# A hybrid decoder layer: the first two weight tiles as one item, loads in a fixed order, joined final sums, and a longer distance from transposes to products

## The chip, the core and the metric

The kernel runs on one core of a Trainium2 chip. The metric is the device time of one execution in microseconds (us). A difference of about 0.2% can be told from no change.

The core's engines are TensorE (PE in the profile, its weight loads PEld), VectorE (DVE), ScalarE (ACT), GpSimd (POOL) and SyncE (SP). Each works through its own queue in order. Transfers are issued on a queue of SP, ACT or POOL and carried out by 16 DMA engines.

## The reference, cut to what matters

One layer (DEPTH = 1) on a residual stream x of 512 tokens by 1024 features, all in float32:

```
proj   = x @ w_in                       # q, k, v of three mixers, and three gate vectors
o_da   = differential attention         # 4 heads, two softmax maps each, RMSNorm per head
o_sb   = stick-breaking attention       # 8 heads, cumulative sums of log sigmoid(-z)
o_dl   = dilated window attention       # 3 groups x 4 heads, joined by their denominators
merged = sum_i sigmoid(gate_i) * (o_i @ w_branch_i)
x1     = LayerNorm(alpha * x + merged @ w_out)
hid    = square(relu(x1 @ w_up))        # 4096 wide
out    = LayerNorm(alpha * x1 + hid @ w_down + sigmoid(x1 @ w_ple_gate) * (p @ w_ple))
```

## The kernel before, in words

**Precision.** Each float32 operand of a large product is split in a rounded high part (h) and the rest (lo). A product is three matmuls: h by h, h by lo, lo by h. The high part is a copy on ScalarE (line 209 for weights), the rest a subtraction on VectorE (line 210). `split_psum`, `evac_stacked` and `evac_twice` (lines 100 to 133) do the same for results in PSUM; line 108 is their subtraction.

**Items.** The program is a list of items. An item has weight chunks, a function that issues its matmuls (`mm`) and one that evacuates the result (`ev`). The main loop (lines 1166 to 1201) issues, for item n: the evacuation of item n-1, some splits, a step of the attention heads, the matmuls of item n with another step in the middle, more splits. Matmul results take turns in two PSUM banks (`mm_bank`); heads, transposes and kept sums use six others (`at_bank`).

A `t_item` (line 243) makes 128 columns of the projection transposed: 24 matmuls of 512 columns. A group of four `v_items` makes values, token tile by token tile, 24 matmuls each, from four chunks. The order is that of `main_order`: two tiles sb_q 0 and sb_k 0, two tiles sb_q 1 and sb_k 1, the values sb_v, then the rest; three gate tiles of column group j are placed two groups ahead of the branch items that use them.

**Weights.** `load` and `fill` (lines 146 to 183) put 512 KB loads on SP's queue into a ring of four raw buffers. `issue_split` splits a chunk into one of seven pairs of buffers (`RING`). `pump(limit, most)` issues up to `most` splits, as far as the count of freed chunks allows. A chunk counts as freed by the item that is its last reader. x is loaded as eight pieces of 256 KB. The first tile's weights come as pieces of 128 KB and 384 KB between them, the second tile's as one chunk behind them.

**Heads.** Heads are generators; each `yield` ends a step, and the main loop calls `step()` twice for most items. So the yields set how many matmuls of items stand between a head's parts. `sb_head` (line 858) does logits (138, 139), ScalarE and VectorE passes (881 to 888), sums by triangular and all-ones matrices (895, 898) and the products with v (917, 919). `da_block` (line 935) does the logits, softmax passes, three yields, transposes (963) and their copy, one yield, the products with v (976); after a head's last block follow the norm, transposes (994) and a split. Before the third item of the first branch group all heads that are left are run to their end without items between (line 1170).

**The end.** The up projection feeds seven blocks of a seven-product scheme (`down`, lines 614 to 656; products 1, 6 and 7 stay in PSUM over all blocks, 2, 3, 4 and 5 are added on VectorE by line 638). The last eighth is done plainly (`plain`, lines 658 to 681): for each of four token tiles and two halves of columns 12 matmuls and an addition (674). After a tile's second half comes its layer norm: `layer_norm_act` (line 420) for tiles 0 to 2, with two sums (425) and two squares (429) on ScalarE, and `layer_norm` (405) for tile 3, with bn_stats on VectorE. Halves are stored on the ACT and SP queues (677).

**Start.** 14 matmuls on zeros (line 734) run first. Constants are made on POOL and cast on VectorE (741 to 758); seven small loads stand on POOL's queue (763, 820 to 838).

Of the kernel before, what the change touches and what calls it, by code (L numbers as in the profile page):

```python
# [17 lines left out]
P = 128  # L18
# [37 lines left out]
def trunk(tc, a, out):  # L56
    nc = tc.nc
    es = ExitStack()
    with es:
# [82 lines left out]
        RING, RAW, NSUM = 7, 4, 3  # L142
        loads, sums, chunks, placed = [], [], [], []
# [24 lines left out]
        def fill():  # L168
            while st["dma"] < len(loads):
                s = loads[st["dma"]]  # L170
                if not s["own"]:
                    if len(placed) >= RAW and placed[-RAW]["uses"]:
                        break
                    placed.append(s)
                if s["own"]:
                    s["raw"] = slot("rawx")
                else:
                    r = ring.tile([P, 1024], F32, name=nm("raw"), tag="raw", bufs=RAW)
                    s["raw"] = r[:, :s["w"]]
                nc.sync.dma_start(s["raw"], s["src"])  # L180
                st["dma"] += 1
                add()
            add()
# [12 lines left out]

        def issue_split():
            c = chunks[st["split"]]
# [8 lines left out]
            for h, lo, a0, a1 in parts:  # L207
                raw = c["from"]["raw"][:, a0:a1]
                nc.scalar.copy(h, raw)  # L209
                nc.vector.tensor_sub(lo, raw, h.bitcast(F32))  # L210
# [32 lines left out]
        def t_item(nt, name, j):  # L243
            w = a["wt"][nt]
            if nt == 0:
                x_chunk(0)
                c0 = chunk(w[:, 0:2, :].rearrange("p k m -> p (k m)"), 256)
                x_chunk(1)
                c1 = chunk(w[:, 2:8, :].rearrange("p k m -> p (k m)"), 768)
                for i in range(2, 8):  # L250
                    x_chunk(i)
                cs = [c0, c1]
            else:
                cs = [chunk(w.rearrange("p k m -> p (k m)"), 1024)]

            def mm(ps):
                for k in range(8):
                    c = cs[0] if nt or k < 2 else cs[1]
                    s = slice(k * P, k * P + P) if nt or k < 2 else slice(k * P - 256, k * P - 128)
# [3 lines left out]

            def ev(ps):
# [21 lines left out]
            item(cs, mm, ev)  # L286
# [33 lines left out]
        nt = nv = 0  # L320
        order = main_order()
        for kind, name, j in order:
# [24 lines left out]
        def branch_items(j):  # L347
            c1 = chunk(a["wb1"][j].rearrange("p k m -> p (k m)"), 1024)
            c2 = chunk(a["wb2"][j].rearrange("p k m -> p (k m)"), 512)
            for n, i in enumerate((1, 2, 0)):  # L350
                def mm(ps, i=i):
# [23 lines left out]
        first_branch = [None]  # L375
        LEAD = 2
# [6 lines left out]
        for j in range(8):  # L383
            branch_items(j)
            if j + LEAD < 8:
                for i in range(3):
                    t_item(nt, "gate", 8 * i + j + LEAD)
                    nt += 1
# [31 lines left out]
        def layer_norm_act(ts, g, b, fin):  # L420

            sm, sq = small("lsm", 2), small("lsq", 2)
            junk = slot("junk")
            for h in range(2):
                nc.scalar.activation(junk, ts[h], AF.Copy, accum_out=sm[:, h:h + 1])
# [129 lines left out]
        def mlp_items():  # L555
# [102 lines left out]
            def plain(cs):  # L658

                for tt in range(4):  # L660
                    for half in range(2):
                        def mm(ps, tt=tt, half=half):
                            q = slice(tt * P, tt * P + P)
                            for i in range(4):
                                h, lo = left[4 * nb + i]
                                c = cs[i % 2, half]
                                s = slice((i // 2) * 512, (i // 2) * 512 + 512)
                                nc.tensor.matmul(ps, h[:, q], c["h"][:, s], start=i == 0, stop=False)
                                nc.tensor.matmul(ps, h[:, q], c["l"][:, s], start=False, stop=False)
                                nc.tensor.matmul(ps, lo[:, q], c["h"][:, s], start=False, stop=i == 3)  # L670

                        def ev(ps, tt=tt, half=half):
                            t = acc[tt, half]
                            nc.vector.tensor_add(t, t, ps)
                            if half:
# [3 lines left out]
                                norm = layer_norm if tt == 3 else layer_norm_act  # L679
                                norm([acc[tt, 0], acc[tt, 1]], "ln2_g", "ln2_b", fin)  # L680
                        item(list(cs.values()) if (tt, half) == (3, 1) else [], mm, ev, need=list(cs.values()))
# [3 lines left out]
            for b in range(nb):  # L685
# [17 lines left out]
                down(b, 3, 0, c3)  # L703
                down(b, 1, 1, c1, [c1, cu])
                down(b, 6, 0, c6)
                down(b, 3, 1, c3, [c3])
# [3 lines left out]
                down(b, 2, 0, c2)  # L710
                down(b, 6, 1, c6, [c6, cu])
                down(b, 2, 1, c2, [c2])
# [3 lines left out]
                down(b, 4, 0, c4)  # L716
                down(b, 7, 0, c7)
                down(b, 7, 1, c7, [c7])
                down(b, 4, 1, c4, [c4])
            wd = a["wd"][nb]  # L720
            plain({(i // 2, i % 2): chunk(wd[i].rearrange("p k n -> p (k n)"), 1024) for i in range(4)})
# [11 lines left out]
        for i in range(14):  # L733
            nc.tensor.matmul(warm, zero[:, 0:P], zero, start=i == 0, stop=i == 13, skip_group_check=True)
        pump(8, 10)
# [5 lines left out]
        nc.vector.tensor_copy(identb, ident)  # L741
# [5 lines left out]
        nc.vector.tensor_copy(ones_r, ones_f)  # L747
# [4 lines left out]
        nc.vector.tensor_copy(tri_r, tri_f)  # L752
# [5 lines left out]
        nc.vector.tensor_copy(mask_b, mask_f)  # L758
# [4 lines left out]
        nc.gpsimd.dma_start(rel[0:32, :], a["rel"])  # L763
# [54 lines left out]
        lamt = slot("lamt")[:, :256].rearrange("p (a b) -> p a b", a=4)  # L818
        src = a["da_lambda"]
        nc.gpsimd.dma_start(lamt, bass.AP(tensor=src.tensor, offset=src.offset, ap=[[0, P], [64, 4], [1, 64]]))  # L820
        lp = one.tile([P, 2], F32, name="lp")
        for i in range(2):
            nc.vector.scalar_tensor_tensor(lamt[:, 2 * i, :], lamt[:, 2 * i, :], 1.0, lamt[:, 2 * i + 1, :],
                                           op0=OP.mult, op1=OP.mult, accum_out=lp[:, i:i + 1])
        nc.scalar.activation(lp, lp, AF.Exp)
        nc.vector.tensor_sub(lam, lp[:, 0:1], lp[:, 1:2])
        nc.vector.tensor_scalar(lam, lam, LAM_INIT, -1.0, op0=OP.add, op1=OP.mult)
        gcol = one.tile([P, 1], F32, name="gcol")
        nc.gpsimd.dma_start(gcol, a["da_norm"])
        nc.vector.tensor_scalar(gcol, gcol, 1.0 - LAM_INIT, None, op0=OP.mult)  # L830
        fold = one.tile([P, P], F32, name="fold")
        foldT = one.tile([P, P], F32, name="foldT")
        nc.gpsimd.dma_start(fold, a["perm"][:, 0:P])
        nc.gpsimd.dma_start(foldT, a["perm"][:, P:2 * P])
        exf = one.tile([P, 8], F32, name="exf")
        nc.gpsimd.dma_start(exf, a["exf"][:, 0:8])
        pick = one.tile([P, 64], F32, name="pick")
        nc.gpsimd.dma_start(pick, a["exf"][:, 8:72])
# [19 lines left out]
        def sb_head(hd):  # L858
# [18 lines left out]
            for bi in (2, 1, 0):  # L877
# [5 lines left out]
                nc.scalar.activation(e, e, AF.Ln, bias=1.0)  # L883
# [4 lines left out]
                nc.vector.tensor_sub(lo, e, h.bitcast(F32))  # L888
# [32 lines left out]
            if 4 + pr not in oT:  # L921
# [4 lines left out]
            if side:  # L926
# [8 lines left out]
        def da_block(hd, qb):  # L935
# [31 lines left out]
            while ("da_v", 0, qb) not in V:  # L967
                yield
            if hd not in da_po:
# [196 lines left out]
        for n, it in enumerate(items):  # L1166
# [3 lines left out]
            if n == first_branch[0] + 2:  # L1170
# [7 lines left out]
            pump(freed)  # L1178
            if n == 14:
                tables()  # L1180
            if n == 22:
# [9 lines left out]
            step()  # L1191
# [5 lines left out]
            pump(freed)  # L1197
# [101 lines left out]
```

## Time and profile before

| | us |
|---|---|
| median of 3 runs (lowest, highest) | 1098.25 (1098.18, 1098.45) |
| the profiled execution, its own time | 1097.73 |
| its span in the profile | 1095.7 |
| PE, DVE, ACT, POOL busy | 1079.6, 676.9, 482.2, 34.5 |
| DMA: bytes, mean rate | 105.71 MB, 96 GB/s |
| PE busy from 220 to 360 us | 140.0 of 140 |
| PE busy from 730 to 1060 us | 330.0 of 330 |
| PE busy from 0 to 25 us | 20.7 of 25 |
| PE busy from 1060 to 1096 us | 25.6 of 36 |

A timeline row has the start (us from the span's start), the duration, engine, line, operation, output<-inputs, shapes and a count; in brackets the idle time before it and what ended it. Matmuls overlap in the rows: one of 512 columns is listed with 0.39 us, while the next starts 0.227 us later. A row of the list of waits has the waiting engine and line, the one waited for, the total in us, how often, and the longest. A row of stretches has the stretch, its length, for PE, PEld, DVE, ACT and POOL the busy time and the number of instructions, the granted clock of TensorE (1.00 is full), the DMA share and GB/s.

### The profile page before, as it was taken

The numbers are of one execution on the slowest core, as the hardware profiler recorded it, in microseconds if no ns is written. First come the engines' busy times: TensorE is split into PE (matmuls) and PEld (weight loads), VectorE is DVE, ScalarE is ACT, GpSimd is POOL, SyncE is SP. The second block draws the span as 40 slices with busy tenths as digits, with TensorE's granted clock in tenths as the row PEclk, the third lists the DMA queues.
The fourth block names the chain that finished last, engine by engine and source line by source line (L and its number), as shares of the span: only waits on it lengthen the run. The fifth ranks groups of instructions, "written<-read, shape, count | busy, mean of one in ns | idle before, by whom it ended". The sixth has DMA issues, their size and how long they took to land.

```text
span 1095.7 us, 13124 instructions
## 1 busy us (share of the span) xinstructions
PE 1079.6 (99%) x5032; PEld 898.3 (82%) x5032; DVE 676.9 (62%) x1192; ACT 482.2 (44%) x803; POOL 34.5 (3%) x62
## 2 busy tenths in 40 slices
PE   8999999999999999999999999999999999999996
PEld 5888788999888888888888888888888888888885
DVE  7868466564253758754444463866686686686676
ACT  6656454343232536553332331333554454454533
POOL 2000200000000000000000020110000000000000
PEclk9999999999999999999999999999999999999999
DMA  7322422121322113222233253253232422332302
GB/s 277 100 96 85 136 77 77 40 96 41 114 77 77 59 39 106 68 76 89 87 96 106 87 181 127 79 175 107 83 96 81 131 97 89 124 97 95 116 1 77
DMA packets 31326, 105.71 MB, mean 96 GB/s; under 512 B 3962, under 2 KB 4106, under 8 KB 31264
## 3 DMA queue, kind: packets, MB, share of 16 engines
q1 hardware_dynamic: 28080, 96.48, 26.8%
q0 software_dynamic: 2608, 7.35, 2.2%
q10 hardware_dynamic: 576, 1.05, 0.3%
q8 instruction: 39, 0.64, 0.2%
q14 instruction: 23, 0.19, 0.1%
HBM read 102.74 MB, written 2.12 MB: 96 GB/s over the span
## 4 chain that ended last, share of the span: by engine, by line
PE 92%; DVE 4%; ACT 2%; DMA 1%; issue 1%; SPq 1%; POOL 0%; DVEq 0%; ACTq 0%
PE mm L87 17%; PE mm L89 17%; PE mm L88 17%; PE mm L299 3%; PE mm L301 3%; PE mm L300 3%; PE mm L632 2%; PE mm L633 2%; PE mm L631 2%; PE at L632 2%; PE at L633 2%; PE at L631 2%; PE mm L462 1%; PE mm L460 1%; PE mm L528 1%; PE mm L526 1%
## 5 line engine op out<-in xcount | busy, mean ns | idle before, releaser
L209 ACT CAST wh<-raw 128x1024 fp32r<-128x1024 f32 (+2 forms) x176 | 180.7, 1028 | 291.6 <-PE mm L88 232.2
L210 DVE TENSOR_TENSOR wl<-raw,wh 128x1024 fp32r<-128x1024 f32 (+2 forms) x176 | 208.8, 1191 | 118.9 <-ACT wh L209 116.6
L87 PE MATMUL mm<-xhT,wh 128*128 128x512 f32 x512 | 202.9, 396 | 1.3 <-ACT xhT L209 1.2
L88 PE MATMUL mm<-xlT,wh 128*128 128x512 f32 x512 | 200.3, 391 | 0.8 <-DVE xlT L210 0.8
L89 PE MATMUL mm<-xhT,wl 128*128 128x512 f32 x512 | 200.4, 391 | 0.5 <-DVE wl L210 0.5
L88 PEld LDWEIGHTS mm<-xlT,wh 128*128 128x128 f32 x512 | 96.2, 188 | 21.1 <-DVE xlT L210 2.0
L87 PEld LDWEIGHTS mm<-xhT,wh 128*128 128x128 f32 x512 | 96.3, 188 | 20.9 <-ACT xhT L209 2.0
L89 PEld LDWEIGHTS mm<-xhT,wl 128*128 128x128 f32 x512 | 96.1, 188 | 20.7 <-DVE wl L210 1.0
L87 PE MATMUL mm<-x1hT,wh 128*128 128x512 f32 x256 | 99.6, 389 | 0.0
L88 PE MATMUL mm<-x1lT,wh 128*128 128x512 f32 x256 | 99.6, 389 | 0.0
L89 PE MATMUL mm<-x1hT,wl 128*128 128x512 f32 x256 | 99.6, 389 | 0.0
L299 PE MATMUL mm<-wh,xhT 128*128 128x512 f32 x160 | 65.5, 410 | 0.0
L300 PE MATMUL mm<-wl,xhT 128*128 128x512 f32 x160 | 63.2, 395 | 0.0
L301 PE MATMUL mm<-wh,xlT 128*128 128x512 f32 x160 | 63.1, 394 | 0.0
L87 PEld LDWEIGHTS mm<-x1hT,wh 128*128 128x128 f32 x256 | 48.0, 188 | 10.1
L88 PEld LDWEIGHTS mm<-x1lT,wh 128*128 128x128 f32 x256 | 48.0, 188 | 10.0
L89 PEld LDWEIGHTS mm<-x1hT,wl 128*128 128x128 f32 x256 | 48.1, 188 | 9.9
L209 ACT CAST wh<-wsum 128x1024 fp32r<-128x1024 f32 x28 | 29.5, 1055 | 52.5 <-PE mm L88 49.3
L210 DVE TENSOR_TENSOR wl<-wsum,wh 128x1024 fp32r<-128x1024 f32 x28 | 34.2, 1222 | 23.8 <-ACT wh L209 23.2
L638 DVE TENSOR_TENSOR xn<-xn,mm 128x512 f32<-128x512 f32 x56 | 38.1, 680 | 9.9 <-PE mm L633 9.8
L631 PE MATMUL mm<-wh,hh 128*128 128x512 f32 x112 | 43.6, 389 | 0.0
L632 PE MATMUL mm<-wl,hh 128*128 128x512 f32 x112 | 43.6, 389 | 0.0
(302 smaller groups left out, 1937.7 us busy)
## 6 DMA issues: line engine op xcount, KB each, us to landing
raw<-in_wt_dram SPq DMA_DIRECT2D x63, 512.0 KB, 3.4
raw<-in_wu_dram SPq DMA_DIRECT2D x32, 512.0 KB, 3.4
raw<-in_wd_dram SPq DMA_DIRECT2D x32, 512.0 KB, 3.4
raw<-in_wv_dram SPq DMA_DIRECT2D x20, 512.0 KB, 3.5
raw<-in_wb_dram SPq DMA_DIRECT2D x8, 512.0 KB, 3.3
raw<-in_wo_dram SPq DMA_DIRECT2D x8, 512.0 KB, 3.6
raw<-in_wg_dram SPq DMA_DIRECT2D x8, 512.0 KB, 4.3
rawx<-in_xT_dram SPq DMA_DIRECT2D x8, 256.0 KB, 6.4
```

The costliest lines, as they stand in the source:

```text
L87: nc.tensor.matmul(ps, wh, xh, start=start, stop=False, skip_group_check=True)
L88: nc.tensor.matmul(ps, wh, xl, start=False, stop=False, skip_group_check=True)
L89: nc.tensor.matmul(ps, wl, xh, start=False, stop=stop, skip_group_check=True)
L209: nc.scalar.copy(h, raw)
L210: nc.vector.tensor_sub(lo, raw, h.bitcast(F32))
L299: nc.tensor.matmul(ps, x1, c["h"][:, s], start=k == 0, stop=False)
L300: nc.tensor.matmul(ps, x1, c["l"][:, s], start=False, stop=False)
L301: nc.tensor.matmul(ps, x2, c["h"][:, s], start=False, stop=k == 7)
L631: nc.tensor.matmul(ps, h[:, q], c["h"][:, s], start=go, stop=False, skip_group_check=True)
L632: nc.tensor.matmul(ps, h[:, q], c["l"][:, s], start=False, stop=False, skip_group_check=True)
L633: nc.tensor.matmul(ps, lo[:, q], c["h"][:, s], start=False, stop=end, skip_group_check=True)
L638: nc.vector.tensor_add(t, t, ps)
```

## The change

The edits, by place:

1. The first two tiles become one item. The x pieces and the two tiles' weights (five loads, k step by k step, from a new array in that layout) alternate, and for each k step six matmuls go to two `at_bank` banks in turn. All 13 splits are issued at once. The first 17 loads are tied one behind the other in SP's order. 9 warm-up matmuls instead of 14. The heads take no step before item 2.
2. Up to item 10 at most one split is issued with each item. Splits between two points are tied behind the first head's last logarithm and subtraction. The constants' casts are tied behind a split, the seven small loads go to SP's queue behind item 4's evacuation, and what is computed of them comes at item 10.
3. `da_block` gets one more yield ahead of the products with v. The three gate tiles ahead move in between the second and the third item of the first branch group, so the third item, and the point at which the heads are run to their end, come three tiles later.
4. In the last block the products 2, 3 and 4 are not done on their own: their 36 matmuls go into the same banks as the plain sums, and their three chunks are freed there. Tile 3 uses `at_bank` banks; its second half is done in two parts of 256 columns.
5. The sums of the last layer norms come from the addition (`accum_out`) for tiles 0 to 2; tile 3 takes bn_stats part by part, and stores in three parts.

The core of the diff:

```diff
+                if 0 < st["dma"] < ORDERED:            # ORDERED = 17
+                    with tc.issue_after(st["load"]):
+                        i = nc.sync.dma_start(s["raw"], s["src"])
...
         def issue_split():
+            with ExitStack() as ties:
+                for i in tie:
+                    ties.enter_context(tc.issue_after(i))
+                split_next()
...
+        def first_item():
+            w = a["w0"].rearrange("p k m -> p (k m)")
+            cs = {}
+            for k in range(8):
+                x_chunk(k)
+                if k in (0, 1, 3, 5, 7):
+                    n = 256 if k in (0, 7) else 512
+                    c = chunk_of(load(w[:, 256 * k:256 * k + n], n, True))
+                    for i in range(n // 256):
+                        cs[k + i] = (c, 256 * i)
+            def mm(ps):
+                for k in range(8):
+                    c, o = cs[k]
+                    for i, (m, x) in enumerate((("h", xh), ("l", xh), ("h", xl))):
+                        for t in range(2):
+                            nc.tensor.matmul(ps[t], c[m][:, o + t * P:o + t * P + P], x[k], ...)
+            def ev(ps):
+                for t in range(2):
+                    t_evac(*order[t][1:])(ps[t])
+            item([cs[k][0] for k in (0, 1, 3, 5, 7)], mm, ev, bank=lambda: (at_bank(), at_bank()))
...
             for n, i in enumerate((1, 2, 0)):          # branch_items(j, between)
+                if n == 2:
+                    for t in between:
+                        t_item(*t)
+                    if j == 0:
+                        first_da.append(len(items))
...
-            for h in range(2):                         # layer_norm_act
-                nc.scalar.activation(junk, ts[h], AF.Copy, accum_out=sm[:, h:h + 1])
...
+                ends = [(0, slice(0, 512)), (1, slice(0, 256)), (1, slice(256, 512))]
+                def part(tt, half, cc):                # plain(cs, c2, c3, c4)
+                    r = tt % 2
+                    p, cp = {(0, 0): (2, c2), (0, 1): (3, c3), (1, 0): (4, c4)}.get((tt // 2, half), (0, None))
+                    def mm(ps):
+                        for i in range(2 if p else 0):
+                            h, lo = left[2 * nb - 2 + i, p]
...
+                            nc.vector.scalar_tensor_tensor(t, t, 1.0, ps, op0=OP.mult, op1=OP.add,
+                                                           accum_out=sums[tt][:, half:half + 1])
...
+                        nc.vector.tensor_add(t[:, cc], t[:, cc], ps[:, :n])
+                        nc.vector.bn_stats(s6[:, ends.index((half, cc)), :], t[:, cc])
...
+                if b < nb - 1:                         # and so for 2, 3 and 4
+                    down(b, 3, 0, c3)
...
-        for i in range(14):
+        for i in range(9):
...
-        pump(8, 10)
+        pump(8, 13)
...
+        pump(8, 1)
+        with tc.issue_after(st["low"]):
+            sb_consts()
...
+                if hd == 0 and bi == 2:
+                    tie[:] = [getattr(i, "ins", i) for i in (ln, low)]
...
             while ("da_v", 0, qb) not in V:
                 yield
+            yield
...
-            if n == first_branch[0] + 2:
+            if n == first_da[0]:
                 while active or waiting:
                     step()
...
-            pump(freed)
+            pump(freed, 1 if n < 10 else 2)
+            if n == 4:
+                tie.clear()
+                with tc.issue_after(st["load"]):
+                    load_consts()
+            if n == 10:
+                with tc.issue_after(st["low"]):
+                    make_lam()
...
-            step()
+            if n > 1:
+                step()
...
-            pump(freed)
+            pump(freed, 0 if n < 10 else 2)
```

## The prediction, made before the changed kernel had run

> **What bounds the kernel now.** I read the page's first part, then TensorE's waits, then the timeline at both ends and around the longest waits, the stretches of the start, and the built order of both kernels on each engine.
>
> ```profile
> PE 1079.6 (99%) x5032; PEld 898.3 (82%) x5032; DVE 676.9 (62%) x1192; ACT 482.2 (44%) x803; POOL 34.5 (3%) x62
> ```
>
> TensorE is busy throughout, and its matmuls of 512 columns start every 0.227 us nearly everywhere. So work off TensorE is worth something only where TensorE waits, before its first product and behind its last. The list of its waits (total, times, longest) says where:
>
> ```profile
> PE at L734 <- DVE rel L762: 1.3, 1, 1.3
> PE mm L87 <- ACT xhT L209: 1.2, 1, 1.2
> PE at L976 <- ACT da_v L96: 0.8, 1, 0.8
> PE mm L88 <- DVE xlT L210: 0.8, 2, 0.6
> PE at L976 <- DVE wT L98: 0.6, 1, 0.6
> PE mm L89 <- DVE wl L210: 0.5, 1, 0.5
> PE at L138 <- DVE sb_ka L108: 0.5, 1, 0.5
> PE mm L668 <- DVE xn L674: 0.4, 1, 0.4
> PE at L976 <- ACT wT L96: 0.2, 1, 0.2
> ```
>
> Three places remain: the first 25 us, the products L976 of the differential attention, and the end. Timeline rows give the ends of the first two tiles and the end of the kernel (start, duration, then what waited):
>
> ```profile
> 21.53 0.39 PE L89 MATMUL mm<-xhT,wl 128*128 128x512 f32 x1
> ...
> 24.03 0.39 PE L88 MATMUL mm<-xlT,wh 128*128 128x512 f32 x1
> 24.87 0.38 PE L138 MATMUL at<-sb_qa,sb_ka 128*128 128x256 f32 x1 [0.46 <-DVE sb_ka L108]
> ```
>
> ```profile
> 1085.66 0.39 PE L670 MATMUL mm<-wh,hl 128*128 128x512 f32 x1
> ...
> 1088.86 0.69 DVE L408 BATCH_NORM_STATS2 bn<-xn 128x6 f32<-128x512 f32 x1
> ...
> 1091.21 1.41 DVE L417 SCALAR_TENSOR_TENSOR xn<-xn,lr,ln_b 128x512 f32<-128x512 f32 x2
> ```
>
> The two tiles end at 21.53 + 0.23 = 21.76, although their 48 matmuls need 48 x 0.227 = 10.9. The last product's slot ends at 1085.89; VectorE then takes until 1092.62, 6.73 later, and store and close 3.05 more.
>
> **1. First item.** Stretches of 2 us (the last column is GB/s) show how fast the loads come:
>
> ```profile
> 2.00:4.00 2.00, 2.00 (x6) 0.76 (x5) 0.00 (x0) 0.49 (x2) 1.91 (x7) 1.00 0.85 247
> 4.00:6.00 2.00, 2.00 (x7) 0.71 (x5) 0.61 (x3) 0.66 (x2) 1.99 (x6) 1.00 0.77 240
> 6.00:8.00 2.00, 2.00 (x9) 1.09 (x7) 1.20 (x2) 0.66 (x2) 0.53 (x2) 1.00 0.95 316
> 8.00:10.00 2.00, 0.58 (x2) 0.19 (x1) 1.22 (x2) 1.86 (x3) 0.00 (x0) 1.00 1.05 380
> ```
>
> Afterwards it is 368 to 414. Now x and both tiles' weights, 3.15 MB, come first: 0.97 MB by 6 us, 1.6 by 8, the rest at about 0.4 MB per us by 12. The constants (some 0.3 MB) leave POOL's queue and that stretch for SP's, behind item 4; there seven small issues of about 0.4 us stand ahead of weight loads split several items early, so I cost them at nothing. The tie of the loads only fixes an order that SP nearly had: nothing. The first x and its weights are the 0.39 MB that are in at 4.41 now; the weight cast (0.40) lets TensorE start near 5.0, where nine warm-up matmuls of 0.427 end too (1.26 + 3.84 = 5.1). The second step needs 0.92 MB (near 6), two casts and two subtractions (0.62 and 0.69 each), so it runs from 7.7 to 9.2. From then a step's data (0.39 MB, 1.0 us) comes faster than its six matmuls run (1.36): six steps more end at 17.4. Against 21.76 that is 4.35 earlier; the wait at L138 (0.84 between starts less 0.23 = 0.6) has its cover too, since the k tile is then evacuated under the third tile. Together 5.0.
>
> **But VectorE does not come 5 us earlier.** In the built order TensorE goes on with the third tile (5.45) and two matmuls, to 23.3; two heads' logits (1.81 and 1.74 in the timeline), 22 matmuls, the first token tile of sb_v (5.45) to 37.3, three blocks of sums (2.3) to 39.6; then the second token tile needs the bank of the fourth tile, whose evacuation L108 is far down VectorE's queue. There stand, from the first head's e (24.05 logits, 0.2, three ScalarE passes of 1.9: 26.1): two heads' first e, cast and subtraction (0.72 + 0.46 + 0.61 = 1.79 each, 3.6), six weight subtractions (1.26 from start to start, 7.6), the third tile's two L108 and two casts (2.3), the 384-wide e (1.45) and the fourth tile's L108 (1.4): 16.3, until 42.4. TensorE waits 39.6 to 42.4, in two or three pieces: 2.7. The start is worth **5.0 - 2.7 = 2.3**. Bounds: 5.0, if ScalarE and VectorE interleave better than I stacked them; 0, if the first item runs late.
>
> **2. Two steps from transposes to products; last blocks before the da branch.** The starts around the three L976 waits leave 0.98, 0.73 and 0.36 more than a matmul's slot. One more yield puts 2.72 us (12 matmuls) or more between each transpose copy or da_v copy and its reader; a copy takes 0.44 to 0.6. The last head's flush gets three gate tiles of 5.45 ahead of it. The last transposes and their split still stand ten matmuls ahead of their reader, as before. **2.1**; bounds 0 (the wait comes back elsewhere) and 3.0 (with small waits of 0.1 to 0.17 there).
>
> **3. Joined products.** 36 matmuls move from the last block into the final sums: 8.2 us of TensorE, moved and not saved. Six L638 additions (0.68) go; VectorE was not waited for there. What they cost: c2, c3, c4 stay in the ring of 7, so the last four weight chunks wait for buffers of products just done. Counted from the end of the third-last up tile: the chunk wd2 is free at 6.8, ready at about 9.2 (1.05 + 1.23 and a queue), read at 11.6; wd3 free at 9.5, ready 12.0, read 15.7. Nothing while slack is 2.4 or more; a bare split costs about 3.0.
>
> **4. The end.** ScalarE's two sums L425 per tile (0.63 + 0.19 each) become an accumulation in the addition. No row has that at 512 columns; between 0.71 (L437, no accumulation) and 0.69 + 0.25 I take 0.85, near L437 with the 0.08 read of L823. The last half goes in two of 256, 24 matmuls of 0.118 for 12 of 0.227: +0.1. The third tile ends 18 and 24 short matmuls before the last (6.9); its norm from L427 to the last L437 took 1077.43 to 1082.39, 4.96, so VectorE is free 0.95 before the last slot ends (0.2 + 0.85 + 4.96 = 6.0). Then in its order: addition 512 (0.7), addition 256 (0.42, L312's row), bn 0.70 and 0.38, which ends 1.3 after the last slot; addition and bn 256 0.85, aggregate and add 0.5, then 1.32 to the pow's return and 0.71 + 0.40 + 0.40: 5.5 instead of 6.73. **1.2**; bounds 0 and 2. The last store is half as long; I take 0, since 256 KB now take 2.1 from issue to landing. The Trainium skill, DMA: Bandwidth & Descriptors, section on the anatomy of one DMA (gpsimd path), has 2.0 us plus bytes over 436 GB/s; by that the half store would be an estimated 0.3 less, and 256 KB would take 2.6, which the row denies. The wait at L668 goes with the banks of tile 3 (start to start 0.58 and 0.11 over): **0.7**, less 0.1.
>
> **Sum.** 2.3 + 2.1 + 1.2 + 0.7 - 0.1 = 6.2. The profiled execution took 1097.73 (span 1095.7), the median is 0.5 above it: 1091.5 there, **1092.0** as median.
>
> **Rivals.** (a) VectorE keeps up in the first 60 us: the full 5.0 and 1089.3. For: its idle gaps of 0.7 around 28 to 32 us; against: it then runs without a gap until 50. (b) The start gives nothing: the clock. Ten warm-up matmuls ran 0.427 apart, until 5.5, and the eleventh 0.216; now the ninth ends at 5.1 and the real ones come in bursts. If three steps run at 0.427 (2.56 each, 5.1 to 12.8 instead of 10.6), the first item ends over 2 later: 1094.3. Against: 1.4 us of waiting at 7.9 did not slow the next ones. The Trainium skill, TensorE: Matmul & The Clock Gate, section on what is actually happening, says that a free-running window of 3.4 us opens the gate only when busy, which speaks for this one; the trace agrees with the size, 4.2 us to the change. (c) The products of v wait elsewhere, or VectorE's end is no shorter: 1094. (d) **Slower:** the ring starves. If the last four splits, tied to products just done, slip past their readers by more than their 2.4 us slack, each bares 3.0; from the third on that eats the 6.2, four with their queues give 1100 to 1104. Against: ScalarE's splits wait for TensorE now too (232 us of L209's idle), and from 730 to 1060 TensorE is busy for all 330 us. (e) The tie does not order anything new: in the sum already.
>
> **Chances.** Forecast 0.50, (a) 0.16, (b) 0.14, (c) 0.12, (d) 0.08. 0.2% is 2.2 us, about what can be told here from no change: faster 0.87, within 0.05, slower 0.08. The range reaches from the best start with some of the bounds, 1088.6, over (b) and (c) to 1095.4, and leaves (d) out.
>
> **What would show it.** First item: its last matmul near 17.4; a wait before the second sb_v token tile near 40, on VectorE's L108 or subtractions; none at L138. No da product waiting over 0.3. From the last matmul to VectorE's end 5.5. No wait for a weight split in the last 45 us. Wrong, if matmuls 0.427 apart go on past 8 us, or if a weight chunk is waited for near the end.

## The result and the profile after

| | before | after |
|---|---|---|
| median of the runs (lowest, highest) | 1098.35 (1098.18, 1099.63) | 1092.82 (1091.29, 1093.94) |
| ratio to before, 95% interval | | 0.9946 [0.9929, 0.9963] |
| the profiled execution, its own time | 1097.73 | 1093.85 |
| its span | 1095.7 | 1092.1 |

The forecast was 1092.0, in a range from 1088.6 to 1095.4. The total is right. The stages it is made of are not, and most of what follows is about that. The four runs lie in two pairs, 1091.29 and 1091.80 at a granted clock of 0.998, 1093.85 and 1093.94 at 0.997 and 0.996, and the forecast falls between them, where no run lies.

To see where the time went I cut the profiled execution at two products that stand in both kernels: A, the start of the last product with dl_v (L1117 before, L1232 after), and B, the start of the first product with pThl (L507, L548). C is VectorE's end.

| stage | before | after | gained | forecast |
|---|---|---|---|---|
| start to A | 378.24 | 379.47 | -1.23 | 2.3 |
| A to B (the differential attention) | 275.93 | 273.29 | 2.64 | 2.1 |
| B to C (the end) | 438.45 | 436.00 | 2.45 | 1.8 |
| C to the execution's own time | 5.11 | 5.09 | 0.02 | 0 |

The start lost where it should have gained. The page's first part, and the list of TensorE's waits of the kernel after (total, times, longest):

```profile
PE 1078.9 (99%) x5039; PEld 901.4 (83%) x5039; DVE 674.6 (62%) x1197; ACT 478.4 (44%) x795; POOL 31.0 (3%) x55
```

```profile
PE at L1008 <- DVE spl L998: 1.6, 2, 1.4
...
PE at L314 <- ACT wh L223: 1.5, 1, 1.5
PE at L831 <- DVE rel L865: 1.3, 1, 1.3
...
PE mm L333 <- DVE sb_kb L108: 0.6, 1, 0.6
...
PE at L1077 <- DVE lg L1072: 0.2, 1, 0.2
```

The waits of L976 (now L1091), L138 and L668 are gone. Two new ones stand at L1008 and L333, with a small one at the transposes L1077, and the first item still waits at L314. The list does not show a third loss, since at half clock TensorE counts as busy. These are the table products and the stretches behind them (the column after the counts is the granted clock):

```profile
109.92 2.75 PE L871 MATMUL at<-oh,rel 33*4 33x512 f32 x10
112.60 0.74 PE L88 MATMUL mm<-xlT,wh 128*128 128x512 f32 x1
```

```profile
110.00:112.00 2.00, 2.00 (x8) 0.59 (x9) 0.00 (x0) 0.89 (x3) 0.11 (x1) 1.00 0.78 262
112.00:114.00 2.00, 2.00 (x8) 1.20 (x6) 0.00 (x0) 1.00 (x3) 2.00 (x5) 0.67 0.04 7
114.00:116.00 2.00, 2.00 (x6) 1.62 (x5) 0.00 (x0) 0.00 (x0) 1.20 (x3) 0.50 0.03 6
116.00:118.00 2.00, 2.00 (x12) 1.64 (x12) 0.00 (x0) 0.00 (x0) 2.00 (x3) 0.97 0.63 135
```

From 112.69 to 116.10 the granted clock is 0.50, and products of 512 columns start 0.427 us apart. From the first table product to A the kernel takes 269.55 here; before, with the same work and a clock of 1.00 there, it took 267.90. So this execution loses 1.65 behind the tables (the kernel with the old start, below, loses it too), and without it the start would be worth 0.42, the same 0.42 by which the table products come earlier (109.92 after 110.34).

The end (VectorE, then TensorE's last product):

```profile
1081.46 1.42 DVE L478 SCALAR_TENSOR_TENSOR xn<-xn,lr,ln_b 128x512 f32<-128x512 f32 x2 [0.65 <-POOL lr L474]
1082.79 1.01 DVE L742 TENSOR_TENSOR xn<-xn,at 128x512 f32<-128x512 f32 x2
1083.72 1.01 DVE L743 BATCH_NORM_STATS2 bn6e<-xn 128x6 f32<-128x512 f32 x2
1084.65 0.41 DVE L742 TENSOR_TENSOR xn<-xn,at 128x256 f32<-128x256 f32 x1
1085.09 0.43 DVE L743 BATCH_NORM_STATS2 bn6e<-xn 128x6 f32<-128x256 f32 x1
...
1085.89 1.40 DVE L760 SCALAR_TENSOR_TENSOR xn<-xn,mv,ln_g 128x512 f32<-128x512 f32 x2
1087.22 1.54 DVE L763 SCALAR_TENSOR_TENSOR xn<-xn,lr,ln_b 128x512 f32<-128x512 f32 x3
```

```profile
1083.83 0.28 PE L727 MATMUL at<-wh,hl 128*128 128x256 f32 x1
```

The last slot ends at 1083.83 + 0.12 = 1083.95, VectorE at 1088.76: 4.81 instead of 6.73.

### The profile page after: what moved, and what is told of

It reads as the page before. It is cut to its first block, busy times and chain, and to the rows that moved or that the text cites. A ratio compares the mean times of both kernels' runs of the same rounds, so it can differ in the third digit from the quotient of the medians.

```text
span 1092.1 us, 13135 instructions
## 1 busy us (share of the span) xinstructions
PE 1078.9 (99%) x5039; PEld 901.4 (83%) x5039; DVE 674.6 (62%) x1197; ACT 478.4 (44%) x795; POOL 31.0 (3%) x55
## 4 chain that ended last, share of the span: by engine, by line
PE 95%; DVE 3%; DMA 1%; ACT 1%; issue 0%; SPq 0%; POOL 0%; DVEq 0%; ACTq 0%
PE mm L87 17%; PE mm L88 17%; PE mm L89 17%; PE mm L333 3%; PE mm L335 3%; PE mm L334 3%; PE mm L672 2%; PE mm L674 2%; PE mm L673 2%; PE at L672 2%; PE at L674 2%; PE at L673 2%; PE mm L567 1%; PE mm L503 1%; PE mm L501 1%; PE mm L568 1%
## 5 line engine op out<-in xcount | busy, mean ns | idle before, releaser
L223 ACT CAST wh<-raw 128x1024 fp32r<-128x1024 f32 (+1 forms) x173 | 178.3, 1031 | 288.7 <-PE mm L88 229.4
L224 DVE TENSOR_TENSOR wl<-raw,wh 128x1024 fp32r<-128x1024 f32 (+1 forms) x173 | 206.2, 1197 | 123.5 <-ACT wh L223 119.7
L87 PE MATMUL mm<-xhT,wh 128*128 128x512 f32 x496 | 196.5, 396 | 0.0
L89 PE MATMUL mm<-xhT,wl 128*128 128x512 f32 x496 | 194.7, 393 | 0.0
L88 PE MATMUL mm<-xlT,wh 128*128 128x512 f32 x496 | 194.5, 392 | 0.0
L88 PEld LDWEIGHTS mm<-xlT,wh 128*128 128x128 f32 x496 | 93.6, 189 | 18.3 <-issue 0.4
L87 PEld LDWEIGHTS mm<-xhT,wh 128*128 128x128 f32 x496 | 93.5, 189 | 18.2
L333 PE MATMUL mm<-wh,xhT 128*128 128x512 f32 x160 | 65.6, 410 | 0.6 <-DVE sb_kb L108 0.6
L224 DVE TENSOR_TENSOR wl<-wsum,wh 128x1024 fp32r<-128x1024 f32 x28 | 34.2, 1222 | 24.2 <-ACT wh L223 23.6
L333 PEld LDWEIGHTS mm<-wh,xhT 128*128 128x128 f32 x160 | 38.0, 237 | 4.2 <-issue 0.8
L335 PEld LDWEIGHTS mm<-wh,xlT 128*128 128x128 f32 x160 | 38.0, 237 | 3.9
L334 PEld LDWEIGHTS mm<-wl,xhT 128*128 128x128 f32 x160 | 38.2, 239 | 3.3
```

The lines of the kernel that those rows point to most:

```text
L87: nc.tensor.matmul(ps, wh, xh, start=start, stop=False, skip_group_check=True)
L88: nc.tensor.matmul(ps, wh, xl, start=False, stop=False, skip_group_check=True)
L89: nc.tensor.matmul(ps, wl, xh, start=False, stop=stop, skip_group_check=True)
L224: i = nc.vector.tensor_sub(lo, raw, h.bitcast(F32))
L333: nc.tensor.matmul(ps, x1, c["h"][:, s], start=k == 0, stop=False)
L334: nc.tensor.matmul(ps, x1, c["l"][:, s], start=False, stop=False)
```

## The experiments

All twelve kernels are the changed one with one edit or a few. Theory: the start is worth 0.4, because the first item ends 1.45 later than forecast and VectorE's queue then holds TensorE up by 2.94 (start to start); parts 3 to 5 carry the gain. Rivals: the start is worth 2.3 as forecast, or the other parts gained less than the stages say. A second theory came with the runs: the clock decides which of several times a run takes.

### One part undone at a time

**The old start.** Parts 1 and 2 taken back, the rest kept.

```diff
-        nt, nv = 2, 0
-        first_item()
+        nt = nv = 0            # two first tiles, 14 warm-ups, constants, pump and ties as before
```

> The changed kernel with its parts 1 and 2 undone (two first tiles, 14 warm-ups, no ties, constants as before); parts 3 to 5 stay. Theory from the trace of after: the start is worth only 0.4 us, because the first item ends at 18.6 instead of 17.4 and 2.9 us of waits for VectorE follow at 39 to 44; so this kernel is only 0.4 us slower than the undisturbed runs of after (1091.3 to 1091.8), about 1092, and it keeps the full clock after the table products near 110 us (granted clock 1.00 from 112 to 118), so that it is even faster than the runs of after with 1093.9. Rival, as predicted: the start is worth 2.3, and this kernel takes 1094 or more. Rival on the clock: the drop after the table products comes here too, and has nothing to do with the start.

Measured: 1093.79 (1092.72 to 1094.96), ratio 0.996 [0.9948, 0.9973]. Its profile has A at 379.77, 0.30 after the changed kernel's, and its clock too falls behind the tables:

```profile
112.00:114.00 2.00, 2.00 (x8) 1.06 (x7) 0.00 (x0) 1.28 (x4) 1.75 (x4) 0.87 0.04 7
114.00:116.00 2.00, 2.00 (x6) 1.60 (x5) 0.00 (x0) 0.00 (x0) 1.28 (x3) 0.50 0.04 7
116.00:118.00 2.00, 2.00 (x10) 1.57 (x10) 0.00 (x0) 0.00 (x0) 2.00 (x4) 0.78 0.48 104
```

So the start is worth 0.3 with the drop in both, 0.42 against before. By these stages the rival of 2.3 falls. The medians, 1093.79 against 1092.82, are 1.0 apart and cannot decide it, since the granted clock differs from run to run in both kernels (0.996 to 0.999). My expectation that the drop belongs to the new start falls too.

**The old differential attention.** Part 3 taken back.

```diff
-            yield              # the extra one in da_block
-            branch_items(j, gs if j == 0 else ())
+            branch_items(j)    # gate tiles behind the group, heads run to their end at first_branch + 2
```

> The changed kernel with part 3 undone (no extra yield ahead of the products with v, gate tiles and the end of the heads where they were). Theory: the waits of products with v and their small gaps come back, 2.1 to 2.6 us: 1093.5 to 1096.5, by the state of the clock near 112 us. Rival: the waits were paid for elsewhere, and it takes the same as after, 1091.3 to 1093.9.

Measured: 1095.7 (1093.46 to 1096.19), 0.9968 [0.9956, 0.9979]. In the list of this kernel's waits the three of before are back, to the tenth:

```profile
PE at L1082 <- ACT da_v L96: 0.8, 1, 0.8
...
PE at L1082 <- DVE wT L98: 0.6, 1, 0.6
...
PE at L1082 <- ACT wT L96: 0.2, 1, 0.2
```

A to B takes 275.95 (before 275.93, after 273.29): 2.66, paid nowhere else, since B to C stays at 435.97.

**The old end.** Parts 4 and 5 taken back.

```diff
-                         bank=at_bank if tt == 3 else None)
-            plain({...}, c2, c3, c4)
+            plain({...})       # products 2, 3, 4 in down(); halves of 512; sums of the norm on ScalarE
```

> The changed kernel with parts 4 and 5 undone (products 2, 3 and 4 of the last block on their own, final sums in halves of 512, sums of the norm on ScalarE). Theory: 6.7 us from the last slot of TensorE to VectorE's end instead of 4.8, and a wait of 0.4 to 0.7 before the last tile: 2.3 us slower, 1093.6 to 1096.2. Rival, as predicted: 1.2 + 0.7 - 0.1 = 1.8. Rival 2: the joined products cost something at the ring, and the difference is below 1.

Measured: 1093.89 (1093.0 to 1095.64), 0.9962 [0.995, 0.9975]. B to C takes 438.48 (before 438.45): 2.48, and the wait of before is back:

```profile
1081.34 0.50 PE L711 MATMUL mm<-wh,hh 128*128 128x512 f32 x1 [0.42 <-DVE xn L717]
```

The medians of these two cannot be set against the changed kernel's 1092.82, because the start went otherwise in the profiled executions. Both have the same start as after, to the instruction, and yet in both the first item ran at half clock for 3.4 us, from 9.88 and from 10.73 on:

```profile
8.00:10.00 2.00, 1.07 (x3) 0.62 (x4) 1.78 (x3) 1.83 (x4) 0.00 (x0) 0.97 1.04 400
10.00:12.00 2.00, 2.00 (x6) 1.54 (x5) 2.00 (x4) 1.83 (x4) 0.00 (x0) 0.50 1.07 394
12.00:14.00 2.00, 2.00 (x7) 1.60 (x7) 2.00 (x4) 1.91 (x4) 0.00 (x0) 0.68 1.02 372
```

(These are stretches of the kernel with the old differential attention; in after the clock is 1.00 in all three.) Their last products of the first item start at 20.23 and 20.30, after's at 18.62. On the other hand neither lost the clock behind the tables: 267.95 from the tables to A in both. So there are two places where the clock may fall or not, and stages, not medians, tell the parts apart.

### VectorE's queue at 40 us

In after TensorE stops three times there:

```profile
41.20 0.39 PE L1008 MATMUL at<-spl,tri_r 128*128 128x256 f32 x1 [1.43 <-DVE spl L998]
...
42.66 0.44 PE L1008 MATMUL at<-spl,tri_r 128*128 128x384 f32 x1 [0.15 <-DVE spl L998]
...
44.18 0.47 PE L333 MATMUL mm<-wh,xhT 128*128 128x512 f32 x1 [0.60 <-DVE sb_kb L108]
```

and this is what VectorE does ahead of them:

```profile
32.91 3.50 DVE L224 TENSOR_TENSOR wl<-raw,wh 128x1024 fp32r<-128x1024 f32 x3
36.44 0.69 DVE L994 SCALAR_TENSOR_TENSOR e<-at,e 128x512 f32<-128x512 f32 x1
37.05 1.22 DVE L224 TENSOR_TENSOR wl<-raw,wh 128x1024 fp32r<-128x1024 f32 x1
38.18 0.42 DVE L997 CAST sph<-e 128x512 fp32r<-128x512 f32 x1
39.32 1.23 DVE L224 TENSOR_TENSOR wl<-raw,wh 128x1024 fp32r<-128x1024 f32 x1 [0.72 <-ACT wh L223]
40.47 0.68 DVE L998 TENSOR_TENSOR spl<-e,sph 128x512 fp32r<-128x512 f32 x1
```

The last of the three L224 at 32.91 and the two behind it are splits of chunks that items 7, 8 and 9 read, over 20 us later; the one at 39.32 even stands waiting for ScalarE, which waits for the load. They are between an e and its own spl because the built order puts them there.

**Late splits.** They are issued later and tied behind the evacuations.

```diff
+            if 2 < n < 8:
+                tie[:] = st["evac"]        # the last evacuation's instructions
+            elif n == 8:
+                tie.clear()
-            pump(freed, 1 if n < 10 else 2)
+            pump(freed, 0 if 2 < n < 5 else 1 if n < 10 else 2)
```

> The changed kernel, but the three weight splits that stand before the first head's sums on VectorE and are read only from item 7 on (5 us or more later) are tied behind the evacuations of items 2 to 6 and spread one by one. Theory (VectorE's backlog): 3.7 us leave VectorE's queue before the subtraction at 40.5, and the waits of 2.9 us at 39 to 44 go: 1088.5 to 1089 where the clock stays full near 112 us, 1091 where it drops. Rival 1: VectorE is full until 50 us whatever the order, and the waits come back at 45 to 60: no better than after. Rival 2: the late chunks are waited for at items 7 to 9: slower by 1 to 3.

Measured: 1094.96 (1093.14 to 1095.55), 0.9965 [0.9953, 0.9978]: no better than after (its median lies 2.1 above), and still the theory holds in its place. The waits at 39 to 44 are 0.0. Its first item was late by a half clock, which alone leaves 2.1 to 2.5 of them (the three other executions with this first item and a half clock), and the later kernel with late splits and mixed tables has 0.0 without it. What it lost came at 122 (TensorE first, then ScalarE):

```profile
125.09 0.62 PE L1032 MATMUL at<-ah,sb_v 128*128 128x512 f32 x1 [2.50 <-DVE ah L1022]
```

```profile
122.40 1.04 ACT L224 CAST wh<-raw 128x1024 fp32r<-128x1024 f32 x1 [4.01 <-PE mm L88]
123.35 0.59 ACT L1019 ACTIVATE a<-at 128x512 f32<-128x512 f32 x1
```

A split that needs the buffer of the item just running stood ahead of a head's exponential, for which TensorE then waited; 2.7 us, and behind that pause the clock was half from 125.31 to 128.72. Neither rival had named this.

**One tie only.** Which of the two, order or clock, matters was then asked with a single tie: the split of sb_v's first chunk goes behind the evacuation of the first item.

```diff
+            if n == 1:
+                tie[:] = st["evac"]
```

> The changed kernel with one split (the chunk of the first sb_v product) tied behind the evacuation of the first item on VectorE, as it stands in the run with zeros; no zeros, nothing else. In the built order the first head's logits then follow 21 products of the third tile instead of 26 (17 in the run with zeros). It tells apart why the zeros gave 2.3 us: Theory A (order): the heads' chain on ScalarE and VectorE starts 1.1 us earlier, and the waits at 39 to 44 (2.9 in after) fall to 1.2 to 1.8, also without zeros; where the clock falls in the first item, the gain is hidden, else 1 to 1.5 us to the end: 1090 to 1093. Theory B (clock): the gain came from the clock of the first item alone, the waits at 39 to 44 stay at 2.1 to 2.9, and the time is that of after, 1091.3 to 1093.9.

Measured: 1090.06 (1089.66 to 1090.28), 0.9921 [0.9909, 0.9933]. The logits start at 23.47, behind 21 products of the tiles (24.74 and 26 in after). VectorE comes to spl at 38.41 instead of 40.47, and of the three stops two are left, 1.11 together:

```profile
40.60 0.44 PE L1010 MATMUL at<-spl,tri_r 128*128 128x384 f32 x1 [0.15 <-DVE spl L1000]
...
42.11 0.47 PE L334 MATMUL mm<-wh,xhT 128*128 128x512 f32 x1 [0.60 <-DVE sb_kb L108]
```

Theory A holds, by more than it had expected: the place of one split, which also lets the logits start five products earlier, is worth 1.8 of the 2.94, without zeros. A comes at 375.82, 2.0 before after's without its drop (379.47 - 1.65 = 377.82).

### The first item and the clock

**A smaller second piece of weights.**

```diff
-                if k in (0, 1, 3, 5, 7):
-                    n = 256 if k in (0, 7) else 512
+                if k in (0, 1, 2, 4, 6):
+                    n = 256 if k < 2 else 512
```

> The changed kernel with the first item's weights in pieces of 256, 256, 512, 512, 512 columns instead of 256, 512, 512, 512, 256: the second step waits for 128 KB less (0.5 us at 240 GB/s) and for a cast of 256 columns instead of 512. Theory: the wait after the first step, 1.6 to 2.3 us in the four profiles with this start, becomes 0.8 to 1.6, the first item ends 0.5 to 0.9 earlier, and of that 0.3 to 0.8 reaches the end: 1090.7 to 1093.5. Rival: the next piece (256 KB) is late in its place, and the first item ends as before. Rival 2: VectorE's backlog at 40 us takes all of it: waits at 39 to 44 longer by what the first item gains.

Measured: 1091.77 (1091.15 to 1095.28), 0.9942 [0.993, 0.9954]. The second step starts at 7.20 instead of 8.92, the next piece is late by 0.7, and the first item's last product starts at 18.04, 0.58 earlier. The waits at 39 to 44 grow to 3.39: 0.45 of the 0.58 is taken there. Rival 2 was right; A (377.74) is 0.1 better than after's without its drop.

**Zeros in the gap.**

```diff
                 for k in range(8):
                     c, o = cs[k]
+                    for i in range(6 if k == 1 else 0):
+                        nc.tensor.matmul(warm, zero[:, 0:P], zero, start=True, stop=True, ...)
```

> The changed kernel with six more products on zeros (1.3 us at full clock) between the first and the second step of the first item, where TensorE waited 1.6 to 2.3 us. Theory (clock): the half clock at 9 to 12.7 us in three of four profiles with this start (not in after's own) comes from that wait; with the gap filled no products run 0.427 apart beyond 8.5 us, and the first item ends at 18.5 to 19.0 instead of up to 20.3. Rival: the clock still drops, as the window saw the half-idle start before; then products 0.427 apart appear between 8 and 13 us. No theory expects more than 0.8 us at the end, since VectorE's waits at 39 to 44 shrink by as much as the first item is late (2.1 and 2.5 where the clock fell, 2.9 where it did not).

Measured: 1090.53 (1090.02 to 1091.38), 0.9925 [0.9913, 0.9937]. The clock stays at 1.00 from 8 to 14, the first item's last product starts at 18.45. But no theory had expected over 0.8, and it gained 2.3. The built order had moved as well: the logits follow 17 products instead of 26 and start at 22.98, and the waits at 39 to 44 are 0.26. Behind the tables this profile lost the clock again, from 110.79 to 114.21. The experiment with one tie above, which has this order in part and no zeros, shows that most of it was the order. What the zeros do for the clock is not settled by it.

**Mixed tables.** The ten table products in four groups of two to four, put between the full products of item 13.

```diff
-            if n == 13:
-                tables()
+            if n == 10:
+                tab = tables()             # a generator now: loads, then two or four products per step
+            if n in (10, 13):
+                next(tab)
...
+                if k in (0, 1, 2) and n == 13:
+                    next(tab, None)        # after each k step of item 13
```

> The changed kernel with its ten small products of the bias tables (33 partitions, 4 columns of weights, 2.75 us in one piece near 110 us) put between the full products of item 13, one table product at a time; their inputs are loaded three items earlier. Theory (clock): half speed for some 3.4 us after the tables, as in after (112.6 to 116.1) and in the kernel with the old start (113.0 to 116.6), comes from the piece of 2.75 us with little activity; mixed in, the granted clock stays 1.00 from 105 to 125, the stage from the tables to the last products with dl_v takes 267.9 as in the runs without the drop (269.5 with it), and the runs lie closer, 1091 to 1092.5, apart from drops in the first item. Rival: the drop has another cause (the heads' small products behind it), and still comes: 0.5 for 3.4 us between 110 and 120.

Measured: 1093.31 (1091.98 to 1093.92), 0.9946 [0.9933, 0.9959]. In this profile the clock holds behind the tables:

```profile
110.00:112.00 2.00, 2.00 (x8) 0.74 (x7) 1.69 (x4) 1.04 (x2) 0.32 (x1) 1.00 0.57 193
112.00:114.00 2.00, 2.00 (x8) 0.61 (x6) 0.00 (x0) 0.72 (x2) 1.20 (x3) 1.00 0.20 75
114.00:116.00 2.00, 2.00 (x9) 1.06 (x9) 0.00 (x0) 0.72 (x2) 0.51 (x1) 1.00 0.03 5
```

but the switches between the two kinds of products cost some 0.7 us together: what the starts leave over between 100 and 150 us is 1.69 where it was 0.98 without a drop. And this execution fell to half clock in the first item. No gain: 0.7 paid in every run against 1.65 in some. That mixing keeps the clock up is not shown by this alone, since most of the profiles with the tables in one piece kept it as well.

### Together

> Late weight splits as in the earlier run, mixed tables, and up to item 24 no split is issued that has to wait for the item just issued (in the earlier run one of them stood before the last head's exponential on ScalarE, and TensorE waited 2.7 us at 122 and lost the clock for 3.4 us behind it). Theory: the waits at 39 to 44 stay away, the one at 122 goes and the clock stays: the last product with dl_v is reached at 376 to 377 instead of 378.2 (before), 379.5 (after) and 380.6 (late splits alone); 1089 to 1090.5 in all. Rival: another wait of a head for ScalarE or VectorE comes in between 60 and 250 us, and it is no better than after, 1091.3 to 1093.9.

> Late splits, mixed tables and the six zero products in one kernel. Theory: no half clock in the first item nor at the tables, no waits at 39 to 44 and none at 122: 1089.0 to 1090.2 with runs less than 1 apart. Rival: the zeros delay the second step where the data come early, and give nothing beyond the late splits (1090.5, 1089.5 to 1092.2 there).

> As the one before, with the tables in one piece as in after. Theory: two groups of runs, 0.7 us below the kernel with mixed tables where the clock stays (the mixing cost 0.7 us in small gaps, by the sum of the starts between 100 and 150 us: 1.69 against 0.98), and 1.0 above it where it falls (1.65): 1088.3 to 1090.9. Rival: no drop in any run, as the phase of the window is set by the first item and the zeros fix it: 1088.3 to 1089.5 throughout.

> Late splits, mixed tables, the smaller second piece of weights, and three zero products instead of six. Theory: the second step starts 0.7 earlier than with the pieces of the change, so the first item ends near 17.9, and since VectorE is not behind any more, all of it reaches the end: 0.5 to 0.7 below the kernel with all three and the old pieces, 1088.4 to 1089.6. Rival: in the built order the logits come after all 24 products of the third tile (17 in the other two), so that the heads' chain starts later and the first product with the sums waits; no gain.

The edit that is new in these (otherwise those shown):

```diff
-            pump(freed, 0 if n < 10 else 2)
+            pump(freed - (len(it["c"]) if n < 24 else 0), 0 if n < 10 else 2)
```

| kernel | median (lowest, highest) | ratio [95%] | waits 39 to 44 | A |
|---|---|---|---|---|
| late splits, mixed tables | 1090.54 (1089.48, 1092.21) | 0.9928 [0.9916, 0.9940] | 0.0 | 376.15 |
| with zeros | 1090.33 (1090.04, 1090.62) | 0.9924 [0.9911, 0.9936] | 0.0 | 375.90 |
| zeros, tables in one piece | 1089.85 (1089.27, 1091.10) | 0.9917 [0.9904, 0.9931] | 0.0 | 376.69, clock fell behind the tables |
| three zeros, small piece, mixed tables | 1089.81 (1089.25, 1090.08) | 0.9918 [0.9905, 0.9932] | 0.0 | 375.67 |

The wait at 122 is gone in all four, so the blocked split was its cause. With tables in one piece one run of five lies 1.1 to 1.8 above the others, and its granted clock is 0.996 against 0.998; its rival, no drop in any run, is out. The four are 0.7 to 0.8% faster than before, and their medians 2.3 to 3.0 below that of after; between them and the kernel with one tie (1090.06), whose waits are 1.1 longer, the intervals decide nothing. The smaller piece did not do what was expected of it: the second step started at 7.07, but the third then waited 1.5 for its own 256 KB piece, and the last product of the first item starts at 18.68 (18.40 with six zeros and the old pieces). Why its median lies 0.5 below that of the kernel with six zeros and mixed tables is open.

## Why the prediction was right in sum and wrong in its parts

**The first item** was to end at 17.4 and ended at 18.85. The failing step is the arrival of the second step's data, "0.92 MB (near 6)": the fourth load landed at 8.22. In all ten profiles with these pieces it landed at 7.98 to 8.30. I had added up the rate from the start of the span: 0.88 MB had moved by 6, and by 8.2 some 1.5 MB, much of it of later loads. The loads are in flight together, and the tie orders their issue, not their landing: the second x piece, issued at 1.72, landed at 7.5 with a 256 KB piece of weights behind it, and at 6.2 with a piece of 128 KB. The size behind it is not the whole cause, since in before the same piece, issued at 1.71, landed at 5.9 with 384 KB behind it; what else decides stays open. Then come the cast and the first product at 8.92:

```profile
6.79 0.67 PE L314 MATMUL at<-xlT,wh 128*128 128x512 f32 x2
8.92 0.73 PE L314 MATMUL at<-xhT,wh 128*128 128x512 f32 x2 [1.46 <-ACT wh L223]
```

From there seven steps ran without a stop, as forecast (42 slots and 0.4 of small gaps).

**VectorE's queue** was to cost 2.7 at 39.6 to 42.4, and cost 2.94 at 39.6 to 44.2: size and engine right, the place only in part. The forecast let the sums run through and put the wait ahead of the second token tile, on L108; only 0.76 stands there, and 2.2 stand inside the sums, on the subtraction L998. That both begin at 39.6 is luck, because the first item ended 1.45 later than forecast. VectorE came to the fourth tile's `sb_kb` at 43.34, and at 43.05 in before, so what the first item gained did not get past this queue. By its terms the start is 21.76 - 18.85 + 0.6 (L138) - 2.94 = 0.57, and 0.42 by the table products. What I did not see is that this queue is a choice of the built order: three of its splits were not due, and one tie takes 1.8 away. Rival (a), that VectorE keeps up, was therefore wrong for this kernel; in the kernels with late splits its condition holds (waits of 0.0).

**The clock.** Half clock in the first item, rival (b), given 0.14, came in four of the seven profiles with this first item, though not in after's own, and not as the rival had it: the clock was full by 6.5 at the latest in these four and fell behind the pause, between 9.1 and 10.7, instead of staying half from 5.1 to 12.8. Its price was mis-sized: the first item ended 1.2 to 1.7 later, but the waits at 39 to 44 shrank by 0.5 to 0.8, and A came 0.9 to 1.3 later instead of 2.3. The drop behind the tables was in no part of the prediction. It is not new with this change, but nothing in the trace of before showed it.

**The differential attention** gave 2.64 for 2.1. Right; the term counted only the three large waits, and the small gaps around them of 0.1 to 0.17, named as the upper bound of 3.0, went too. No product waits over 0.3 there now; the only wait listed is 0.2 at the transposes L1077, which is new.

**The end** gave 2.45 for 1.8. The addition with accumulation took 0.69 and a read of 0.08, not 0.85, so VectorE was free 1.16 before the last slot's end instead of 0.95, the last addition began 0.70 after it instead of 1.3, and the first pass L760 ran beside POOL's power instead of behind it. That makes 1.92 for the forecast 1.2; the other 0.53 stand for 0.7 less 0.1. The two half stores took 2.02 and 2.06 from issue to landing, where those of 256 KB took 2.03 to 2.14, so the 0 for them was right. (These stores are issued by ACT and SP, so they do not deny the 2.6 that the forecast had estimated for the gpsimd path.) Rival (d) did not come: no weight split was waited for at the end.

So two terms that were 1.2 too small together covered most of a start that was 1.9 too large. Without the drop behind the tables the profiled execution would have gained 5.5 of the 6.2 forecast. The sum came out right for reasons that are half its own, and the rest is luck.

## What to carry to other kernels

Where a start is made faster, look at the queue of the engine that comes next, and at which of its work is not yet due: here the place of a single split was worth 1.8, where the whole rearranged start had left 0.4. Read a forecast against stages, cut at instructions that both kernels have, because a clock that falls in some runs can move the median by as much as an edit does. When prefetch is limited by a ring, see that an early split never has to wait for the item that is running, or all that follows on its engine waits too.

## What the runs showed of the hardware

Between the warm-up and the last product, half speed comes in pieces of one length, 3.41 us: from 112.69 to 116.10 (after), from 113.47 to 116.89 (old start), from 125.31 to 128.72 (late splits), from 9.88 to 13.29 (first item, old differential attention) and from 10.73 to 14.14 (first item, old end). In each trace all changes of the granted clock lie a whole multiple of 3.413 us apart; in after 31 of them lie between 6.87, where the clock first rises, and 112.69. So each trace has a grid with a mark every 3.413 us, and a drop fills one stretch between two marks.

Three things stood ahead of the drops: ten products of 33 rows and 4 columns in 2.75 us during which TensorE is never idle, a pause of 2.7, and a first step followed by a pause of 1.8 to 2.3, where pauses of 1.2, 1.6 and 2.2 in three other executions left the clock alone. Behind the same table products the clock fell in four of ten profiles with the tables in one piece, and in none of four with mixed tables. The grid tells the ten apart: where the clock fell, the tables began 0.07, 0.09, 0.23 and 0.65 us behind a mark of the grid, so that nearly the whole stretch was theirs; in the six others they began 0.74 to 2.59 behind one and ran on into the next stretch. For the pauses the idle time in the stretch just ahead goes the same way, 2.03 to 2.67 us in the five that fell (start to start, less a slot) and 1.57, 1.79 and 2.01 in the three that did not; these lie too close together to call it a limit. No run here was made to test the grid.

The Trainium skill, TensorE: Matmul & The Clock Gate, section on what is actually happening, puts the window at 3.4 us and lets it run free; the length and the grid agree. The Trainium skill, TensorE: Matmul & The Clock Gate, section HAM oscillation, gives as the abstract rule that idle gaps above some 3.4 us are what bites. Here a pause of 2.7 and a busy stretch of 2.75 with little in it were enough, so the measurement decides: shorter gaps, and small products without any gap, can cost 1.2 to 1.7 as well.
